# Second stage of an MLP: the first product's half units dealt out over all groups of the seven-product stage, and that stage's last block product placed among the direct end's first products

## The chip, the core and the metric

The kernel runs on one core of one Trainium2 chip. The metric is the device time of one execution in microseconds. The change touches the last third of the kernel, the MLP; everything ahead of it is the same in both versions.

## The reference, cut to what matters

One layer of a hybrid encoder, 256 tokens of width 2048, in float32: a mixer (two kinds of attention and an RWKV branch) with a residual, and then the MLP that this case is about. Its hidden width is 8192.

```python
x = x + _rms_norm(mix, norm_mix_post[l])
hdn = jnp.square(jax.nn.relu(_rms_norm(x, norm_mlp_pre[l]) @ w_mlp_up[l]))
x = x + _rms_norm(hdn @ w_mlp_down[l], norm_mlp_post[l])
```

`w_mlp_up` is 2048 x 8192, `w_mlp_down` 8192 x 2048.

## The kernel before, in words

**Splitting.** Every weight tile is 128 x 1024 floats (512 KB). It is fetched by the SP queue into a buffer `raw` (tag `raw`, three buffers, for the first product) or `raw2` (six buffers, for the blocks), then split in two: `ScalarE` copies it, rounded, to `whi` (line 152), and `VectorE` subtracts that from the tile to give the rest, `wlo` (line 153). `whi` and `wlo` have three buffers each. After a group or so every fourth tile is split into a spare tile `sp` instead (lines 1074 and 1075), and every seventh block is loaded into a spare tile. TensorE multiplies with the high and the low part.

**First product.** The hidden width is cut into 64 units of 128. A unit takes two weight tiles; its work on one of them is a half unit: eight products with `whi` and eight narrower ones with `wlo` (`gemm`, lines 168, 172 and 176). After the second half, `post` (lines 1101 to 1111) empties the PSUM tile and applies relu and the square.

**Second product.** The units go in five blocks, SIZES = (12, 16, 16, 12, 8), FIRST = (0, 12, 28, 44, 56). Blocks 0 to 3 are multiplied by the seven-product scheme for 2 x 2 block matrices (Winograd's form of Strassen's): in place of eight block products there are seven, named F1 to F7, and sums of blocks. For this the hidden values are brought into seven forms (`forms`, lines 1131 to 1142), and the weight blocks are summed on the way: two such sums are made by VectorE (line 1168) and two by a transfer that adds to its destination, issued by GpSimd (`dma_add`, line 1171). Each of the seven block products takes one split tile and the forms of two pairs of units; on TensorE it is six matmuls (lines 1209 to 1211). The seven over two pairs of units (four units) and one half of the output width are called a group here: blocks 0 to 3 have 3, 4, 4 and 3 groups for each of the two output halves, 28 groups in all, numbered 0 to 27 in this text. Results go from PSUM into `y` by short VectorE additions (line 1216).

The last block, units 56 to 63, is multiplied directly (`tok`, lines 198 and 214): the direct end. Its hidden values are only split (`split3`, lines 1153 and 1154). It reads 16 weight tiles, and ends with the second norm and the residual: `x1`, read back from DRAM (`xs`), is added and written out.

**Order.** Units 0 to 11 are made before group 0. The other 52 units are made during the groups, one block ahead of their use. A list `work` is written by hand; `drive` takes its items one by one, and prepares (`prep`: loads, splits, sums) two items further on than the one that TensorE runs. An item's number says how many small waiting tasks (forms, sums into `y`) go out behind it. In a group the order is F3, half, F4 of the group before, forms that are due, F7, F1, half, F6, F2, half, F5, half. F4 is put off by a group's half because its tile is the one that the second adding transfer makes: loaded tile `R22` is used by F3, F7 and F6 and summed in between, and then `dma_add(R22, R21)` gives F4's tile.

Every group takes two units, four halves, as long as there are any. 52 units are 26 groups' worth, so groups 26 and 27 have none; in them the seven products' items send out one task each. F4 of group 27 (`last4`) is run at the end, and then the first tiles of the direct end are loaded (`first3`). The four gains and the four parts of `x1` are fetched one by one behind the direct end's first weight tiles (list `side`). `x1` lies in the buffers of the two spare tiles, so it can be fetched when these are no longer needed.

In the MLP a scheduler places each engine's instructions by their priority in this order and by what they need; each engine then works its list in order. SP's list too is worked in order: a transfer that has to wait holds those behind it.

```python
for it in (F[3], us[0], last4, "old", F[7], F[1], us[1], F[6], F[2], us[2], F[5], us[3]):
```

Of the kernel before, what the change touches and what calls it, by code (L numbers as in the profile page):

```python
# [10 lines left out]
F32 = mybir.dt.float32  # L11
# [7 lines left out]
D = 2048  # L19
# [31 lines left out]
def hybrid_block(ctx, tc, xt, x, gains, params, consts, lora, gup, wst, out):  # L51
    nc = tc.nc
# [12 lines left out]
    def nm(s):  # L65
        uid[0] += 1
        return f"{s}_{uid[0]}"
# [7 lines left out]
    def pk():  # L75
        return pkpool.tile([128, 512], F32R, tag="pk", name=nm("pk"), bufs=24)
# [20 lines left out]
    threads = []  # L97
# [4 lines left out]
    def start(gen):  # L102

        threads.append({"gen": gen, "need": None, "due": clock[0]})
# [36 lines left out]
    side = []  # L141
# [109 lines left out]
    def g1(w=T):  # L251
        return rp.tile([128, T], F32, tag="g1", name=nm("g1"), bufs=20)
# [46 lines left out]
    for h in range(2):  # L299
        w = {}  # L300
        for k in range(8 * h, 8 * h + 8):
            xsplit(k)
            i = k - 8 * h
            if i in (0, 3, 5):
                j = len(w)
# [537 lines left out]
    for hf in range(2):  # L843
        for s, mo in (("k", MU_K), ("r", MU_R), ("v", MU_V)):
            for p in range(4 * hf, 4 * hf + 4):
                ps = unit(upk)
                d = g1()
# [33 lines left out]
    for g in range(4):  # L881
        m = rp.tile([128, 2, 512], F32, tag="m", name=nm("m"), bufs=4)
        m = [m[:, 0], m[:, 1]]
# [25 lines left out]
    for g in range(4):  # L909
        if g < 3:  # L910
            branch(ycp, thc[g], ms[g], False)
        else:
            m = [pk().bitcast(F32) for _ in range(2)]
# [6 lines left out]
    p2 = ctx.enter_context(tc.tile_pool(name="p2", bufs=1))  # L920
# [23 lines left out]
    x1 = [p2.tile([128, D], F32, tag="x1", name=nm("x1"), bufs=2) for _ in range(2)]  # L944
    for c in range(0, D, 512):
        for tt in range(2):
            loads.append(lambda tt=tt, c=c: nc.sync.dma_start(out=x1[tt][:, c:c + 512],
                                                              in_=x[tt * 128:tt * 128 + 128, c:c + 512]))
# [42 lines left out]
    for k2 in range(0, KT, 2):  # L991
# [7 lines left out]
        for i in range(2):  # L999
            u = pk()  # L1000
# [15 lines left out]
    xs = [dp.tile([128, D], F32, name=nm("xs")) for _ in range(2)]  # L1016
    AF_ = {1: 0, 2: 1, 4: 2, 7: 3, 5: 4, 6: 5, 3: 6}
    SIZES = (12, 16, 16, 12, 8)
    FIRST = [sum(SIZES[:b]) for b in range(5)]
    work, urgent, tasks, hl = [], [], [], {}  # L1020
    ahead, spare, made, kinds, units = [AHEAD], [], [0], [0], [0]

    def emit(n):

        while n and tasks:
            tasks.pop(0)[1]()
            n -= 1
# [226 lines left out]
    def later(new):  # L1254
        return (None, lambda _: urgent.append(lambda: tasks.extend(new)), 0)
# [12 lines left out]

    LAST = FIRST[4] // 2
    old = []  # L1270
    nxt, last4 = SIZES[0], None
    m_new = SIZES[0] // 2
    left = {m: 0 for m in range(m_new, 8)}
    for b in range(4):
        for sb in range(2):
            for d, F in enumerate(down(b, sb)):
                us = []
                while len(us) < 2 and nxt < FIRST[4] + SIZES[4]:
                    us.append(up(nxt))
                    nxt += 1  # L1280
                us = [u for pair in us for u in pair] + [None] * 4
                if not us[0]:
                    F = {f: it[:2] + (1,) for f, it in F.items()}
                for it in (F[3], us[0], last4, "old", F[7], F[1], us[1], F[6], F[2], us[2], F[5], us[3]):
                    if it == "old":
                        keep = []
                        for m in old:
                            if m in left:
                                work.append(later(split3(m) if m >= LAST else forms(m)))
                            else:  # L1290
                                keep.append(m)
                        old[:] = keep
                    elif it:
                        work.append(it)
                if us[3]:
                    old.append(nxt // 2 - 1)
                last4 = F[4]
                if sb:
                    for m in (2 * d, 2 * d + 1):
                        left[FIRST[b] // 2 + m + 8] = 0  # L1300
    work.append(last4)

    def first3():
        order[:] = [base + 3 * 64 + 32 + 8 * g + k for g in range(4) for k in range(4, 8)]
        for _ in range(1 + AHEAD):
# [4 lines left out]
        work.append(later(split3(m)))  # L1310
    work.append((None, lambda _: first3(), 0))
    drive()
    spare.clear()
    x1 = [p2.tile([128, D], F32, tag="x1", name=nm("x1"), bufs=2) for _ in range(2)]

    hp = [hp[k] for k in range(FIRST[4], FIRST[4] + SIZES[4])]
    g4, loads = gain(1, [pk() for _ in range(4)])
    side.extend(loads)
    for tt in range(2):
        side.extend(lambda tt=tt, c=c: nc.sync.dma_start(out=x1[tt][:, c:c + 1024], in_=xs[tt][:, c:c + 1024])  # L1320
                    for c in (0, 1024))
    for g in range(4):
        gs = slice(512 * g, 512 * g + 512)
        for tt, ps in enumerate(tok(hp, 3 if g == 3 else 1)):
            yv = ys[tt][:, gs]
            V.tensor_tensor(yv, yv, ps, ALU.add)
            A.activation(junk(), yv, AF.Square, accum_out=ss4[:, tt, g:g + 1])

            def gained():
                V.tensor_tensor(yv, yv, g4[g], ALU.mult)  # L1330

            if g < 3:
                gained()
                if g == 2:
                    sum4.append(rstd_of(ss4[:, tt, :], eps4[tt], None))
            else:
                r4 = rstd_of(ss4[:, tt, :], None, sum4[tt])
                gained()
                for c in range(0, D, 512):
                    cs = slice(c, c + 512)  # L1340
                    V.scalar_tensor_tensor(x1[tt][:, cs], ys[tt][:, cs], r4, x1[tt][:, cs], ALU.mult, ALU.add)  # L1341
                    nc.sync.dma_start(out=out[tt * 128:tt * 128 + 128, cs], in_=x1[tt][:, cs])
# [125 lines left out]
```

## Time and profile before

| | |
|---|---|
| median of three runs | 1549.11 us (1543.35 to 1551.61) |
| profiled execution | 1545.02 us |
| its span | 1543.2 us |
| TensorE busy | 1506.6 us, 98% |
| VectorE busy | 1194.7 us, 77% |
| ScalarE busy | 918.5 us, 60% |
| read from memory | 281.86 MB |

The profile is of one execution; the 1.8 us between its time and its span lie outside the recorded instructions. In its rows PE is TensorE's matmuls, PEld its weight loads, DVE VectorE, ACT ScalarE, POOL GpSimd, SP the engine that issues most transfers; SPq and POOLq are queues of transfers. L168 is line 168. `mps<-whi,fm` is a matmul that writes a tile `mps` and reads `whi` and `fm`. A row of the timeline has the start in us from the span's start, the duration, the engine, the line, what was written and read, how many there are in the row, and in brackets how long the engine had been idle and what ended that.

In the seven-product stage (about 930 to 1485 us) TensorE's matmuls follow each other without a gap up to 1463 us. Matmuls are pipelined, so that one of 0.39 us starts every 0.23 us.

### The profile page before, as it was taken

How to read it: one execution, taken by the hardware profiler on the slowest of the kernel's cores; microseconds unless marked ns; L12 is line 12 of the kernel's file. 1: busy time of each engine (PE TensorE's matmuls, PEld its weight loads, DVE VectorE, ACT ScalarE, POOL GpSimd, SP SyncE). 2: the span in 40 equal slices, each digit the busy share in tenths (PEclk: the TensorE clock that was granted, in tenths of full speed). 3: DMA queues.
4: the chain of work that ended last, by engine and by line, in shares of the span. 5: the costliest groups of instructions: out<-in, count | busy, mean ns of one | idle time of the engine just before them, and what ended most of it. 6: DMA issues, size and time to landing. Idle time of an engine off the chain costs nothing.

```text
span 1543.2 us, 22386 instructions
## 1 busy us (share of the span) xinstructions
PE 1506.6 (98%) x8294; PEld 1264.1 (82%) x8294; DVE 1194.7 (77%) x1608; ACT 918.5 (60%) x1340; POOL 91.1 (6%) x163
## 2 busy tenths in 40 slices
PE   7999999999999999999999999999999999999987
PEld 6888888888777788788887888888888888888865
DVE  6865567788548798447655878999899989998975
ACT  7564566554546554455444766777667776776642
POOL 0021000000000100000000000000000000000000
PEclk9999999999999999999999999999999999999999
DMA  7545455545534445435785658888888887889864
GB/s 259 189 165 175 153 178 178 167 147 187 176 121 141 160 160 192 154 125 180 241 304 178 232 173 249 250 260 247 255 254 256 254 263 228 255 253 273 255 191 137
DMA packets 105117, 316.88 MB, mean 205 GB/s; under 512 B 10288, under 2 KB 12720, under 8 KB 104624
## 3 DMA queue, kind: packets, MB, share of 16 engines
q1 hardware_dynamic: 93536, 282.76, 53.4%
q0 software_dynamic: 8064, 29.36, 10.3%
q10 hardware_dynamic: 3408, 3.34, 0.6%
q8 instruction: 65, 1.06, 0.3%
q14 instruction: 44, 0.36, 0.1%
HBM read 281.86 MB, written 4.19 MB: 185 GB/s over the span
## 4 chain that ended last, share of the span: by engine, by line
PE 47%; issue 5%; DMA 2%; DVE 1%; ACT 1%; POOL 0%; POOLq 0%; DVEq 0%; ACTq 0%
PE gps L168 12%; PE gps L214 10%; PE gps L172 7%; PE gps L198 3%; PE mps L1209 3%; PE mps L1210 3%; PE mps L1211 3%; PE gps L1209 2%; PE gps L1211 2%; PE gps L1210 2%; DMA raw<-in_wst_dram 1%; PE gps L176 1%; DMA sp<-raw 0%; DMA raw<-sp 0%; DVE x L1341 0%
## 5 line engine op out<-in xcount | busy, mean ns | idle before, releaser
L153 DVE TENSOR_TENSOR wlo<-raw,whi 128x1024 fp32r<-128x1024 f32 x505 | 613.5, 1222 | 193.8 <-ACT whi L152 176.2
L152 ACT ACTIVATE whi<-raw 128x1024 fp32r<-128x1024 f32 x505 | 532.0, 1057 | 273.9 <-PE gps L214 122.8
L168 PE MATMUL gps<-pk,whi 128*128 128x512 f32 x1301 | 330.9, 393 | 0.1
L214 PE MATMUL gps<-whi,pk 128*128 128x512 f32 x1144 | 291.3, 394 | 0.0
L168 PEld LDWEIGHTS gps<-pk,whi 128*128 128x128 f32 x1301 | 241.3, 188 | 48.2 <-issue 0.9
L214 PEld LDWEIGHTS gps<-whi,pk 128*128 128x128 f32 x1144 | 213.6, 188 | 45.6 <-issue 1.0
L172 PEld LDWEIGHTS gps<-pk,wlo 128*128 128x128 f32 x1391 | 190.1, 190 | 14.5 <-issue 1.2
L172 PE MATMUL gps<-pk,wlo 128*128 128x256 f32 x1391 | 195.8, 283 | 0.0
L214 PE MATMUL gps<-wlo,pk 128*128 128x512 f32 x572 | 157.4, 394 | 0.0
L214 PEld LDWEIGHTS gps<-wlo,pk 128*128 128x128 f32 x572 | 106.9, 188 | 23.2 <-issue 0.7
L1075 DVE TENSOR_TENSOR sp<-raw,sp 128x1024 fp32r<-128x1024 f32 x69 | 84.2, 1220 | 3.9 <-ACT sp L1074 3.7
L1101 ACT ACTIVATE sp<-gps 128x512 f32<-128x512 f32 x52 | 31.1, 598 | 88.2 <-PE gps L176 88.1
L1074 ACT ACTIVATE sp<-raw 128x1024 fp32r<-128x1024 f32 x69 | 72.9, 1056 | 16.0 <-PE mps L1210 7.0
L1209 PE MATMUL mps<-whi,fm 128*128 128x512 f32 x168 | 67.0, 399 | 6.9 <-ACT whi L152 6.9
L198 PE MATMUL gps<-whi,pk 128*128 128x512 f32 x264 | 71.9, 393 | 0.0
L1211 PE MATMUL mps<-wlo,fm 128*128 128x512 f32 x168 | 66.2, 394 | 0.8 <-DVE wlo L153 0.8
L1210 PE MATMUL mps<-whi,fm 128*128 128x512 f32 x168 | 66.3, 395 | 0.0
L1171 POOL DMA_DIRECT2D raw<-raw x40 | 35.0, 874 | 439.7 <-DVE raw L1168 137.8
L198 PEld LDWEIGHTS gps<-whi,pk 128*128 128x128 f32 x264 | 49.3, 188 | 10.5 <-ACT whi L152 0.2
L1209 PE MATMUL gps<-whi,fm 128*128 128x512 f32 x126 | 49.3, 391 | 0.0
L1168 DVE TENSOR_TENSOR raw<-raw,raw 128x1024 f32<-128x1024 f32 x40 | 48.8, 1220 | 0.4
L1211 PE MATMUL gps<-wlo,fm 128*128 128x512 f32 x126 | 49.1, 391 | 0.0
(342 smaller groups left out, 1964.9 us busy)
## 6 DMA issues: line engine op xcount, KB each, us to landing
raw<-in_wst_dram SPq DMA_DIRECT2D x502, 512.0 KB, 4.3
raw<-raw POOLq DMA_DIRECT2D x40, 512.0 KB, 6.1
sp<-in_wst_dram SPq DMA_DIRECT2D x16, 512.0 KB, 5.4
raw<-sp POOLq DMA_DIRECT2D x8, 512.0 KB, 6.5
sp<-raw POOLq DMA_DIRECT2D x8, 512.0 KB, 6.9
x<-in_x_dram SPq DMA_DIRECT2D x8, 256.0 KB, 5.9
xs<-x SPq DMA_DIRECT2D x2, 1024.0 KB, 4.0
x<-xs SPq DMA_DIRECT2D x4, 512.0 KB, 5.4
```

The source lines that it names most:

```text
L152: A.activation(hi, raw, AF.Copy)
L153: V.tensor_tensor(lo, raw, hi.bitcast(F32), ALU.subtract)
L168: PE.matmul(ps, hi[:, i * 128:i * 128 + 128], pks[i], start=first and i == 0, stop=False)
L172: PE.matmul(ps[:, 0:T], lo[:, i * 128:i * 128 + 128], pks[i][:, 0:T], start=False, stop=False)
L198: PE.matmul(ps[tt], pks[k][:, c:c + 128], w[:, (k - k0) * 512:(k - k0) * 512 + 512], start=k == 0 and part == 0 and w is hl[0], stop=w is ...
L214: PE.matmul(ps[tt], pks[k][:, c:c + 128], w[:, (k - k0) * 512:(k - k0) * 512 + 512], start=k == 0 and part == 0 and w is hl[0], stop=False)
L1074: A.activation(hi, raw, AF.Copy)
L1075: V.tensor_tensor(lo, raw, hi.bitcast(F32), ALU.subtract)
L1168: V.tensor_tensor(x, x, z, ALU.add)
L1209: PE.matmul(Q[f], p, w, start=d == 0 and i == 0, stop=False)
L1210: PE.matmul(Q[f], pl, w, start=False, stop=False)
L1211: PE.matmul(Q[f], p, wl, start=False, stop=d == nd - 1 and i == 1)
```

## The change

There are as many half units as before (104), and as many of all other instructions. A list `share` says how many halves each group takes: four in the first 18 groups, then 3, 3, 3, 3, 4, 4, 3, 4, 3, 2. So a unit can begin in one group and end in the next; its forms are due in the group after its second half. In the last group all items send out a task.

`last4` is no longer run ahead of the direct end: a thread (`end4`) that advances with the direct end's own count of time prepares it some 3.5 us into the direct end, runs it 3 us later, and sends out its sums into `y` after another 2 us. The spare tiles stay in use until then, and `x1` is fetched in one piece of the program ahead of the direct end's third quarter.

```diff
--- before.py
+++ after.py
@@ -1268,19 +1268,19 @@
 
     LAST = FIRST[4] // 2
     old = []
-    nxt, last4 = SIZES[0], None
-    m_new = SIZES[0] // 2
-    left = {m: 0 for m in range(m_new, 8)}
+    last4 = None
+    left = {m: 0 for m in range(SIZES[0] // 2, 8)}
+    halves = [(h, j) for j in range(SIZES[0], FIRST[4] + SIZES[4]) for h in up(j)]
+    share = [4] * 18 + [3, 3, 3, 3, 4, 4, 3, 4, 3, 2]
+    assert sum(share) == len(halves)
+    halves_of = {j: (h, j) for h, j in halves}
     for b in range(4):
         for sb in range(2):
             for d, F in enumerate(down(b, sb)):
-                us = []
-                while len(us) < 2 and nxt < FIRST[4] + SIZES[4]:
-                    us.append(up(nxt))
-                    nxt += 1
-                us = [u for pair in us for u in pair] + [None] * 4
-                if not us[0]:
-                    F = {f: it[:2] + (1,) for f, it in F.items()}
+                us = [halves.pop(0) for _ in range(share.pop(0))]
+                new = [j // 2 for i, (u, j) in enumerate(us) if j % 2 and (u, j) == halves_of[j]]
+                us = [u for u, j in us] + [None] * 4
+                last = b == 3 and sb == 1 and d == SIZES[3] // 4 - 1
                 for it in (F[3], us[0], last4, "old", F[7], F[1], us[1], F[6], F[2], us[2], F[5], us[3]):
                     if it == "old":
                         keep = []
@@ -1291,15 +1291,12 @@
                                 keep.append(m)
                         old[:] = keep
                     elif it:
-                        work.append(it)
-                if us[3]:
-                    old.append(nxt // 2 - 1)
+                        work.append(it[:2] + (1,) if last and it[2] == 0 else it)
+                old.extend(new)
                 last4 = F[4]
                 if sb:
                     for m in (2 * d, 2 * d + 1):
                         left[FIRST[b] // 2 + m + 8] = 0
-    work.append(last4)
-
     def first3():
         order[:] = [base + 3 * 64 + 32 + 8 * g + k for g in range(4) for k in range(4, 8)]
         for _ in range(1 + AHEAD):
@@ -1310,17 +1307,31 @@
         work.append(later(split3(m)))
     work.append((None, lambda _: first3(), 0))
     drive()
-    spare.clear()
-    x1 = [p2.tile([128, D], F32, tag="x1", name=nm("x1"), bufs=2) for _ in range(2)]
+
+    def end4():
+        yield 3.5
+        hl = last4[0]()
+        yield 3.0
+        last4[1](hl)
+        while urgent:
+            urgent.pop(0)()
+        yield 2.0
+        emit(-1)
+
+    start(end4())
 
     hp = [hp[k] for k in range(FIRST[4], FIRST[4] + SIZES[4])]
     g4, loads = gain(1, [pk() for _ in range(4)])
     side.extend(loads)
-    for tt in range(2):
-        side.extend(lambda tt=tt, c=c: nc.sync.dma_start(out=x1[tt][:, c:c + 1024], in_=xs[tt][:, c:c + 1024])
-                    for c in (0, 1024))
     for g in range(4):
         gs = slice(512 * g, 512 * g + 512)
+        if g == 2:
+            assert not threads
+            spare.clear()
+            x1 = [p2.tile([128, D], F32, tag="x1", name=nm("x1"), bufs=2) for _ in range(2)]
+            for tt in range(2):
+                for c in (0, 1024):
+                    nc.sync.dma_start(out=x1[tt][:, c:c + 1024], in_=xs[tt][:, c:c + 1024])
         for tt, ps in enumerate(tok(hp, 3 if g == 3 else 1)):
             yv = ys[tt][:, gs]
             V.tensor_tensor(yv, yv, ps, ALU.add)
```

Three places where the order of instructions moved. The first is ScalarE's list in group 26, from the split for F7 on (L152 and L1074 are splits; `raw_13465`, `raw_13493`, `raw_13430` and the like are loaded blocks; L1101, L1107 and L1111 belong to `post`, L1153 to `split3`). Before:

```order
L152 ACTIVATE whi_13467<-sp_8489 128x1024
L1101 ACTIVATE sp_8489<-gps_13410 128x512
L1074 ACTIVATE sp_8488<-raw_13465 128x1024
L1107 ACTIVATE tmp_13479<-tmp_13479 128x256
L152 ACTIVATE whi_13495<-sp_8489 128x1024
L1111 ACTIVATE pk_13393<-tmp_13479 128x256
L1153 ACTIVATE fm_13506<-pk_13203 128x256
L152 ACTIVATE whi_13509<-raw_13493 128x1024
L1153 ACTIVATE fm_13519<-pk_13203 128x256
L152 ACTIVATE whi_13522<-raw_13430 128x1024
L1153 ACTIVATE fm_13532<-pk_13393 128x256
L1074 ACTIVATE sp_8488<-raw_13535 128x1024
```

With the change:

```order
L152 ACTIVATE whi_13352<-sp_8489 128x1024
L1074 ACTIVATE sp_8488<-raw_13350 128x1024
L1101 ACTIVATE sp_8489<-gps_13321 128x512
L152 ACTIVATE whi_13390<-raw_13388 128x1024
L1107 ACTIVATE tmp_13383<-tmp_13383 128x256
L152 ACTIVATE whi_13402<-sp_8489 128x1024
L1111 ACTIVATE pk_13313<-tmp_13383 128x256
L152 ACTIVATE whi_13413<-raw_13400 128x1024
L1074 ACTIVATE sp_8488<-raw_13440 128x1024
L1153 ACTIVATE fm_13559<-pk_13313 128x256
L1153 ACTIVATE fm_13572<-pk_13313 128x256
L152 ACTIVATE whi_13450<-raw_13297 128x1024
```

Before, the only splits are those of F7, F1, F6, F2, F5 and the next group's F3; now the splits of half units, `raw_13388` and `raw_13440`, stand between them.

The second is TensorE's list where the seven products end and the direct end (L214) begins. Before, with F4 of group 27 in `mps_13486`:

```order
L1209 MATMUL mps_13486<-whi_13617,fm_12608 128x512
L1210 MATMUL mps_13486<-whi_13617,fm_12611 128x512
L214 MATMUL gps_13668<-whi_13645,fm_12998 128x512 x2
L1211 MATMUL mps_13486<-wlo_13618,fm_12608 128x512
L1209 MATMUL mps_13486<-whi_13617,fm_12898 128x512
L1210 MATMUL mps_13486<-whi_13617,fm_12941 128x512
L1211 MATMUL mps_13486<-wlo_13618,fm_12898 128x512
L214 MATMUL gps_13669<-whi_13645,fm_12998 128x512 x2
L214 MATMUL gps_13668<-whi_13645,fm_13001 128x512 x2
L214 MATMUL gps_13669<-whi_13645,fm_13001 128x512 x2
```

With the change, with F4 of group 27 in `mps_13376`:

```order
L214 MATMUL gps_13654<-whi_13670,fm_13559 128x512 x2
L214 MATMUL gps_13655<-whi_13670,fm_13559 128x512 x2
L214 MATMUL gps_13654<-whi_13670,fm_13572 128x512 x2
L214 MATMUL gps_13655<-whi_13670,fm_13572 128x512 x2
L1209 MATMUL mps_13376<-whi_13681,fm_12829 128x512
L1210 MATMUL mps_13376<-whi_13681,fm_12832 128x512
L1211 MATMUL mps_13376<-wlo_13682,fm_12829 128x512
L1209 MATMUL mps_13376<-whi_13681,fm_12893 128x512
L1210 MATMUL mps_13376<-whi_13681,fm_12896 128x512
L1211 MATMUL mps_13376<-wlo_13682,fm_12893 128x512
L214 MATMUL gps_13654<-wlo_13671,fm_13559 128x512
L214 MATMUL gps_13655<-wlo_13671,fm_13559 128x512
```

F4 stood around the direct end's first matmuls (x2: two equal rows); now it stands in the middle of the direct end's third tile (`whi_13670`, `wlo_13671`), behind 32 of its matmuls.

The third is SP's list of transfers at the same place (L145 the direct end's weight tiles, L1064 blocks, L928 gains, L1320 and L1334 `x1`; `sp_8489` is the block R21 of group 27, loaded into a spare tile). Before:

```order
L145 DMA raw_13682<-in_wst_dram 128x1024
L928 DMA pk_13664<-in_gains_dram 128x512
L928 DMA pk_13665<-in_gains_dram 128x512
L1064 DMA raw_13561<-in_wst_dram 128x2x512
L928 DMA pk_13666<-in_gains_dram 128x512
L928 DMA pk_13667<-in_gains_dram 128x512
L1064 DMA sp_8489<-in_wst_dram 128x2x512
L1320 DMA x_2554_13662<-xs_7783 128x1024 x2
L1320 DMA x_2555_13663<-xs_7784 128x1024 x2
L145 DMA raw_13701<-in_wst_dram 128x1024
L145 DMA raw_13720<-in_wst_dram 128x1024
```

With the change:

```order
L145 DMA raw_13632<-in_wst_dram 128x1024
L928 DMA pk_13650<-in_gains_dram 128x512
L1064 DMA sp_8489<-in_wst_dram 128x2x512
L928 DMA pk_13651<-in_gains_dram 128x512
L928 DMA pk_13652<-in_gains_dram 128x512
L928 DMA pk_13653<-in_gains_dram 128x512
L145 DMA raw_13668<-in_wst_dram 128x1024
L1334 DMA x_2587_13828<-xs_7783 128x1024 x2
L145 DMA raw_13691<-in_wst_dram 128x1024
L145 DMA raw_13716<-in_wst_dram 128x1024
L1334 DMA x_2588_13829<-xs_7784 128x1024 x2
L145 DMA raw_13747<-in_wst_dram 128x1024
```

The four parts of `x1` (two rows of two) stood in one piece behind the direct end's third weight tile, with thirteen tiles behind them; now the first two stand behind the third tile and ahead of the fourth and fifth, and the other two behind those.

## The prediction

> **What bounds the kernel now.** I read the page's head first, then the busy time by stretches, then TensorE's waits, and last the chain of waits and the timeline at the place that these name.
>
> ```profile
> span 1543.2 us, 22386 instructions
> PE 1506.6 (98%) x8294; PEld 1264.1 (82%) x8294; DVE 1194.7 (77%) x1608; ACT 918.5 (60%) x1340; POOL 91.1 (6%) x163
> L153 DVE TENSOR_TENSOR wlo<-raw,whi 128x1024 fp32r<-128x1024 f32 x505 | 613.5, 1222 | 193.8 <-ACT whi L152 176.2
> L1168 DVE TENSOR_TENSOR raw<-raw,raw 128x1024 f32<-128x1024 f32 x40 | 48.8, 1220 | 0.4
> ```
>
> TensorE is the bound of the whole: a change that moves no work off it can win only where it waits. The next rows, from the busy time by stretches, have TensorE, its weight loads, VectorE, ScalarE and GpSimd (time and count), and then the granted clock, the transfer engines' share and GB/s.
>
> ```profile
> 1290.00:1455.00 165.00, 165.00 (x848) 141.30 (x847) 154.84 (x181) 115.24 (x154) 13.93 (x16) 1.00 0.86 251
> 1357.00:1378.00 21.00, 21.00 (x109) 17.98 (x108) 21.00 (x27) 15.14 (x22) 1.74 (x2) 1.00 0.77 224
> 1290.00:1491.00 201.00, 193.00 (x951) 161.75 (x950) 184.49 (x214) 133.04 (x177) 16.54 (x19) 0.98 0.84 244
> 1464.00:1491.00 27.00, 19.04 (x65) 13.37 (x66) 22.78 (x27) 11.04 (x13) 1.74 (x2) 0.87 0.67 184
> ```
>
> From 1290 to 1455, groups 18 to 25, TensorE never pauses though VectorE is busy 94% of the time. From 1464 to 1491, groups 26 and 27 and the first tile of the direct end, TensorE does 65 matmuls in 27 us. All its waits in the MLP from 950 us on are these:
>
> ```profile
> PE mps L1209 <- ACT whi L152: 6.9, 3, 4.2
> PE mps L1211 <- DVE wlo L153: 0.8, 2, 0.5
> PE mps L1209 <- ACT sp L1074: 0.2, 1, 0.2
> ```
>
> ScalarE is named, but the chain of waits says what ScalarE waited for: three transfers.
>
> ```profile
> 1459.71 7.06 DMA sp<-raw
> ...
> 1469.22 4.55 DMA sp<-in_wst_dram
> ...
> 1477.62 5.26 DMA raw<-sp
> ...
> 1482.97 1.06 ACT whi L152
> ```
>
> So in groups without half units, the blocks' loads and the adding transfers come too late: a block product gives TensorE little to do while VectorE splits and sums its tile. The timeline of TensorE shows what a product, a half unit and the long wait cost:
>
> ```profile
> 1448.24 1.98 PE L168 MATMUL gps<-pk,whi 128*128 128x512 f32 x8
> ...
> 1451.01 0.40 PE L1209 MATMUL mps<-whi,fm 128*128 128x512 f32 x1
> ...
> 1452.39 1.75 PE L168 MATMUL gps<-pk,sp 128*128 128x512 f32 x7
> ...
> 1484.07 0.80 PE L1209 MATMUL mps<-whi,fm 128*128 128x512 f32 x1 [4.22 <-ACT whi L152]
> ...
> 1490.78 1.99 PE L214 MATMUL gps<-whi,fm 128*128 128x512 f32 x8
> 1492.61 1.07 PE L214 MATMUL gps<-wlo,fm 128*128 128x512 f32 x4
> 1493.51 0.84 PE L214 MATMUL gps<-whi,fm 128*128 128x512 f32 x3
> ```
>
> A half unit takes 1451.01 - 1448.24 = 2.77 us, a block product 1.38 us. Unhindered, twelve matmuls take 1493.51 - 1490.78 = 2.73 us, 0.2275 each. So 65 would take 14.8 us, and the stretch loses 27.0 - 14.8 = **12.2 us**. Of these 7.9 are the waits listed. Another 2.6 are the slow clock after the longest of them: between 1484.07 and 1490.78 TensorE runs the direct end's first tile and group 27's F4, 18 matmuls, in 6.7 us where 4.1 would do. The remaining 1.7 is the refilling of the matmul pipeline after the waits.
>
> **The change, part by part.** *Half units.* Nothing is added or removed; five halves go from groups 18 to 25 to groups 26 and 27. TensorE's work is the same, and each group's time on it is 7 x 1.38 + 2.77 for each half: 20.7 us with four, 18.0 with three, 15.2 with two, against 9.7 with none. With at least 15.2 us for it, the chain of a group's loads and sums has time again, so the waits go: up to -12.2 us.
>
> What it costs: in a group with three or two halves the work of the seven products comes denser. On VectorE that is nine operations of 1.22 us (seven splits, two sums). The missing half between F5 and the next F3 gave TensorE 2.77 us of work and VectorE one split of 1.22, so it let VectorE get 1.5 us further ahead. How far ahead it is shows where the end of a split is set against the first matmul that reads its low part (VectorE's rows, then TensorE's):
>
> ```profile
> 1398.56 1.22 DVE L1075 TENSOR_TENSOR sp<-raw,sp 128x1024 fp32r<-128x1024 f32 x1
> 1441.40 1.22 DVE L1075 TENSOR_TENSOR sp<-raw,sp 128x1024 fp32r<-128x1024 f32 x1
> 1449.55 1.22 DVE L153 TENSOR_TENSOR wlo<-sp,whi 128x1024 fp32r<-128x1024 f32 x1
> ```
>
> ```profile
> 1400.43 0.39 PE L1211 MATMUL gps<-sp,fm 128*128 128x512 f32 x1
> 1455.63 0.40 PE L1211 MATMUL gps<-wlo,fm 128*128 128x512 f32 x1
> 1457.00 0.39 PE L1211 MATMUL mps<-wlo,fm 128*128 128x512 f32 x1
> ```
>
> F3 of group 26 has 1455.63 - 1450.77 = 4.9 us in hand; F1 of group 23, behind both sums, has 1400.43 - 1399.78 = 0.65, the least I found. With 1.5 less, F3 keeps 3.4, and an F1 like that one is 0.9 late. Six groups have three halves and one has two: from nothing to 7 x 0.9, 0 to 6 us given back. I take 2.5, nearer to nothing: that F1 was the worst one, and only the part of the 1.5 counts that isn't made up before F1. The two-half group has the direct end's products in place of its last halves.
>
> *Forms and splits of the hidden values* move with their units; they are as many, on VectorE and ScalarE, and lie in the sum above. The last unit's `split3` now stands right ahead of the direct end, which needs it only in its fourth tile, three tiles (8.2 us) later: 0.
>
> *The last block product.* Its six matmuls only change their place: 0 on TensorE. It no longer holds the direct end, and the 4.22 us wait and the slow clock behind it go; they are part of the 12.2. Its tile's adding transfer is started when F6 of group 27 is split. From F6 to the product there are F6, F2, F5 and 32 matmuls of the direct end: 3 x 1.38 + 7.3 = 11.4 us. The transfer (5.26 us in the chain above) and the two halves of the split (1.06 and 1.22) need 7.5: hidden, with 3.9 us in hand. Queued behind this split on ScalarE and VectorE is that of the direct end's fourth tile, 0.9 us of matmuls later: if the transfer takes more than 9 us, both are late.
>
> *`x1`.* As many transfers, at another place in SP's list: two of them, and all tiles behind them, now wait for that last adding transfer ahead of the direct end's fourth weight tile.
>
> ```profile
> DMA to landing us min/median/max: 5.2/6.4/10.7
> ...
> raw<-in_wst_dram SPq DMA_DIRECT2D x10, 512.0 KB, 4.1
> x<-xs SPq DMA_DIRECT2D x4, 512.0 KB, 5.4
> ```
>
> The first row is of the adding transfers from 930 to 1460 us, the others of 1470 to 1510. TensorE needs the fourth tile's low part 13.7 us after F6 begins (11.4, F4's 1.38, and 0.9 of products with its high part). The adding transfer lands some 5.3 us after F6 was split, so 8.4 are left, 6.1 without the split. With the two `x1` transfers ahead the tile takes 5.4 us beside them and 5.4 + 4.1 = 9.5 behind them: 0 to 3.4 us late. I take 0: the four `x1` transfers too were issued in one piece, and took 5.4 us each, not four times as long in turn. The gains and the tail after TensorE's last matmul stay: 0.
>
> The Trainium skill speaks against this place: "DMA: Bandwidth & Descriptors", section "Issuing engines are not separate DMA queues", says that transfers started by SP and by GpSimd run on the same 16 engines and interleave. By that the adding transfer would share them with the direct end's tiles and `x1`, as in the busy stretch, where rows above have 10.7 us as the longest; the gain would be some 3 us less, 1542. In the trace the chain's three transfers (4.55 to 7.06) show no such length.
>
> **Sum:** -12.2 + 2.5 = -9.7 us. The profiled execution took 1545.0 us, 4.1 less than the median of the three runs; the sum makes it 1535.3, and the median 1549.1 - 9.7 = **1539.4**. All of the gain would be 1536.9.
>
> **Rivals.** *VectorE becomes the bound.* From 1290 to 1491 it is busy 184.5 of 201 us; without 12.2 the same work stands in 188.8, 98%. For it: no stretch here holds 98% for so long. Against it: 21 us at 100% (second row of the stretches) without a wait. If 94%, its share while TensorE ran freely, is all that goes, the work takes 184.5 / 0.94 = 196.3 us: a gain of 4.7, 1544.4.
>
> *The direct end waits for its fourth tile* behind `x1` or the last split, by up to the 3.4 us above: 12.2 - 2.5 - 3 = 6.7, 1542.4.
>
> *The other side: the adding transfers end last in every short group.* F4's tile is complete when `R21` has been added. In group 25 the transfer could start when F6 was split, at 1442.62, and F4 read its low part at 1457.00: 14.4 us. With one half less between them 11.6 are left, less 2.3 for the split: 9.3 for the transfer. Median 6.4 speaks against a wait; a longest of 10.7, and the denser traffic, for one. A group with four halves moves about 20.7 x 251 = 5.2 MB; a half less is 0.52 MB less, so 4.7 MB in 18.0 us, 260 GB/s. Each us above 9.3 costs the seven short groups 7 us. From a mean of 10.7 on, the 9.7 are lost; at 11.3, 14 - 9.7 = 4.3 us slower, 1553.4; at 11.8, 7.8 slower.
>
> **How the numbers follow.** The forecast 0.64; VectorE as the bound 0.20; the fourth tile 0.08; the adding transfers 0.08, of which 0.05 slower by over 0.5%. The range takes the full gain from the fastest of the three runs, 1543.35 - 12.2 = 1531, and goes up past the VectorE rival to 1547. About 0.5%, 7.7 us, is what a measurement of this kernel can tell from no change. Of the forecast's 0.64, 0.04 give back 4.5 us or more and lie within it; so faster 0.60, within 0.35, slower 0.05.
>
> **What would show it.** Right: no waits of TensorE over 1 us between 1290 us and the end of the direct end, no dip of its clock there, the direct end's first matmul straight behind F5, and a span 8 to 12 us shorter. Wrong: waits at `wlo` in F1 of the three-half groups with VectorE full (first rival); a wait at the direct end's fourth tile with SP held (second); waits at F4 with ScalarE waiting for an adding transfer (third).

## The result, and the profile after

The changed kernel took 1533.1 us (median of six runs, 1531.5 to 1534.5) beside 1548.6 of the kernel before: a ratio of 0.9907, 95% interval 0.9893 to 0.9922, 14.4 us faster. On a second occasion it was 1534.2 beside 1545.9, ratio 0.9923 (0.9909 to 0.9937), 11.7 us. The profiled execution took 1534.53 us.

The head of the page of after:

```profile
span 1532.8 us, 22383 instructions
PE 1503.2 (98%) x8294; PEld 1262.6 (82%) x8294; DVE 1192.7 (78%) x1608; ACT 917.8 (60%) x1340; POOL 91.0 (6%) x163
```

The span is 10.4 us shorter; all engines have the same instructions as before. Two of the stretches that the prediction showed, in after:

```profile
1290.00:1455.00 165.00, 164.16 (x829) 139.09 (x828) 156.88 (x184) 116.27 (x155) 14.99 (x18) 1.00 0.87 253
1464.00:1491.00 27.00, 27.00 (x129) 22.63 (x128) 23.54 (x29) 14.81 (x20) 0.87 (x1) 1.00 0.85 294
```

In the last row 129 matmuls stand where there were 65; the granted clock is 1.00 where it was 0.87, and the transfer engines carry 294 GB/s where they carried 184. TensorE's waits in the MLP are two:

```profile
PE gps L1211 <- DVE wlo L153: 0.4, 1, 0.4
PE mps L1211 <- DVE sp L1075: 0.4, 1, 0.4
```

TensorE's timeline where the direct end begins shows the last F5, the direct end's first tile straight behind it, and F4 of group 27 in the middle of its third, at full speed:

```profile
1476.03 0.39 PE L1211 MATMUL mps<-wlo,fm 128*128 128x512 f32 x1
1476.26 1.98 PE L214 MATMUL gps<-whi,fm 128*128 128x512 f32 x8
...
1483.96 0.39 PE L1211 MATMUL mps<-wlo,fm 128*128 128x512 f32 x1
...
1486.68 0.62 PE L198 MATMUL gps<-wlo,fm 128*128 128x512 f32 x2
```

Where the two waits of 0.4 come from: F2 of group 20 (1339.19) waited for a block that was loaded into the spare tile in 7.98 us, F1 of group 21 (1352.33) for VectorE's own row of a sum and a split. The chain of waits of after, and then VectorE's row behind that block:

```profile
1328.75 7.98 DMA sp<-in_wst_dram
...
1339.19 0.50 PE mps L1211
...
1349.92 1.22 DVE raw L1168
1351.14 1.15 DVE wlo L153
...
1352.33 0.50 PE gps L1211
```

```profile
1337.91 1.23 DVE L1075 TENSOR_TENSOR sp<-sp,sp 128x1024 fp32r<-128x1024 f32 x1 [3.96 <-ACT sp L1074]
```

VectorE had stood 3.96 us for that same block, and then worked almost without a pause (12.70 of the 13 us from 1340 us) up to the second wait.

The theory after the result: the gain is the loss between 1464 us and the end of the direct end's first tile, taken away by the two parts together; what is given back in the short groups is given back through transfers that come late. Rivals: VectorE's load sets what is given back; the last product's place alone brings the gain; part of the 14.4 us lies outside what the profiles show, which have 10.4.

### The profile page after: what moved, and what is told of

It is laid out like the page before. It is cut to its first block, busy times and chain, and to the rows that moved or that the text cites. A ratio compares the mean times of both kernels' runs of the same rounds, so it can differ in the third digit from the quotient of the medians.

```text
span 1532.8 us, 22383 instructions
## 1 busy us (share of the span) xinstructions
PE 1503.2 (98%) x8294; PEld 1262.6 (82%) x8294; DVE 1192.7 (78%) x1608; ACT 917.8 (60%) x1340; POOL 91.0 (6%) x163
## 4 chain that ended last, share of the span: by engine, by line
PE 53%; DVE 1%; DMA 1%; ACT 1%; issue 0%; POOL 0%; DVEq 0%; POOLq 0%; ACTq 0%
PE gps L168 14%; PE gps L214 10%; PE gps L172 8%; PE mps L1209 3%; PE mps L1210 3%; PE mps L1211 3%; PE gps L198 3%; PE gps L1211 2%; PE gps L1209 2%; PE gps L1210 2%; PE gps L176 1%; DMA sp<-in_wst_dram 1%; DVE x L1352 0%; DVE wlo L153 0%; ACT junk L1113 0%
## 5 line engine op out<-in xcount | busy, mean ns | idle before, releaser
L152 ACT ACTIVATE whi<-raw 128x1024 fp32r<-128x1024 f32 x507 | 533.9, 1057 | 276.0 <-PE gps L214 107.7
L214 PE MATMUL gps<-whi,pk 128*128 128x512 f32 x1144 | 291.5, 394 | 0.0
L214 PEld LDWEIGHTS gps<-whi,pk 128*128 128x128 f32 x1144 | 213.7, 188 | 45.8 <-issue 1.0
L214 PE MATMUL gps<-wlo,pk 128*128 128x512 f32 x572 | 157.4, 394 | 0.0
L214 PEld LDWEIGHTS gps<-wlo,pk 128*128 128x128 f32 x572 | 106.9, 188 | 23.2 <-issue 0.7
L1074 ACT ACTIVATE sp<-raw 128x1024 fp32r<-128x1024 f32 x67 | 70.7, 1055 | 14.9 <-PE mps L1211 3.9
L1101 ACT ACTIVATE sp<-gps 128x512 f32<-128x512 f32 x52 | 31.1, 597 | 80.7 <-PE gps L176 80.7
L1209 PE MATMUL mps<-whi,fm 128*128 128x512 f32 x168 | 66.2, 394 | 0.0
L198 PEld LDWEIGHTS gps<-whi,pk 128*128 128x128 f32 x264 | 49.3, 188 | 10.6 <-ACT whi L152 0.2
L1209 PE MATMUL gps<-whi,fm 128*128 128x512 f32 x126 | 49.2, 391 | 0.0
```

Of the source, the lines that this page charges most:

```text
L152: A.activation(hi, raw, AF.Copy)
L198: PE.matmul(ps[tt], pks[k][:, c:c + 128], w[:, (k - k0) * 512:(k - k0) * 512 + 512], start=k == 0 and part == 0 and w is hl[0], stop=w is ...
L214: PE.matmul(ps[tt], pks[k][:, c:c + 128], w[:, (k - k0) * 512:(k - k0) * 512 + 512], start=k == 0 and part == 0 and w is hl[0], stop=False)
L1074: A.activation(hi, raw, AF.Copy)
L1209: PE.matmul(Q[f], p, w, start=d == 0 and i == 0, stop=False)
```

## Experiments

The first four kernels ran beside 1547.4 us of the kernel before, the next four beside 1545.9, the last three, on a third occasion, beside 1545.9. All ratios are to the kernel before of the same occasion. The place of `x1` is as in the change in all of these kernels but the kernel before; no run moves `x1` alone.

**One part alone: the half units spread, the last product ahead of the direct end.**

```diff
+    work.append(last4)
...
-    start(end4())
```

(The body of `end4` goes too.)

> Half units spread as in the change, but the last block product F4 stays ahead of the direct end. Theory: it has to wait there for its adding transfer. From the start of F6 to F4 there are three products, 4.1 us; the transfer (5.3 us in the trace of before) and the split (2.3) need about 7.5. So one wait of about 3.5 us and, if the clock drops again, 2 to 3 us of slow matmuls behind it: about 1539 us, ratio to before 0.993 to 0.995, 4 to 6 us slower than the changed kernel. Rival: with half units in every group all transfers come in time, and the place of the last product is worth nothing: like the changed kernel, 1533 us, 0.991, and no wait of TensorE ahead of the direct end.

1537.5 us, ratio 0.9934 (0.9922 to 0.9947). Its waits of TensorE:

```profile
PE gps L214 <- DVE wlo L153: 0.7, 1, 0.7
PE gps L168 <- DVE junk L1216: 0.6, 1, 0.6
PE mps L1211 <- DVE wlo L153: 0.5, 1, 0.5
```

The ratio is what was expected, but not for the reason given. F4 of group 27 waited 0.5 us; no long wait for its adding transfer came, and no slow clock. With two halves in group 27 the transfer starts early enough even for a product that stands ahead of the direct end: it went out at 1470.5 us, and ScalarE split its tile at 1475.6.

**The other part alone: the last product moved, groups 26 and 27 without halves.**

```diff
-    share = [4] * 18 + [3, 3, 3, 3, 4, 4, 3, 4, 3, 2]
+    share = [4] * 26 + [0, 0]
...
-                last = b == 3 and sb == 1 and d == SIZES[3] // 4 - 1
+                last = not us[0]
```

> Halves as before (none in groups 26 and 27), but the last block product among the direct end's first products. Theory: the waits inside groups 26 and 27 stay (about 3.6 us named in the trace of before, 5 with the refilling of the pipeline), the long one of 4.2 us and the slow clock behind it (2.6) go: about 7 us faster than before, 1541 us, 0.9955, with the adding transfer landing while the direct end's tiles are multiplied. Rival: the long wait only moves, because the last product's split stands in ScalarE's and VectorE's lists ahead of the direct end's fourth tile and its transfer starts as late as before: a wait in the third or fourth tile of the direct end, and 0 to 3 us faster than before, 0.998 to 1.000.

1539.6 us, ratio 0.9950 (0.9937 to 0.9962), near the theory's 1541 and 0.9955.

```profile
PE mps L1209 <- ACT whi L152: 3.3, 3, 1.8
PE mps L1211 <- DVE wlo L153: 1.1, 2, 0.5
PE mps L1209 <- ACT sp L1074: 0.2, 1, 0.2
```

And its last stretch, with columns as before:

```profile
1464.00:1491.00 27.00, 22.76 (x93) 16.93 (x94) 23.64 (x27) 14.38 (x17) 1.74 (x2) 1.00 0.74 210
```

The wait of 4.2 us is gone and with it the slow clock (the clock is 1.00); the waits inside groups 26 and 27 stay, 4.6 us in all.

**Two halves in each of the last four groups**, in place of six groups of three and one of two:

```diff
-    share = [4] * 18 + [3, 3, 3, 3, 4, 4, 3, 4, 3, 2]
+    share = [4] * 24 + [2] * 4
```

> The change with the same 104 halves dealt otherwise: four in groups 0 to 23, two in each of groups 24 to 27. Theory: VectorE has more than a two-half group's 15.2 us of work, so that what it is ahead (3 to 5 us at F3) is used up in four such groups in a row: waits at low parts of F7, F1 and F6 in groups 25 to 27, 2 to 5 us in all, 1535 to 1538 us, 0.992 to 0.994. Rival: only whole groups without halves are too thin, any halves do: like the changed kernel, 1533 us, 0.991, no waits over 0.5 us.

1539.6 us, ratio 0.9947 (0.9934 to 0.9959), slower than either expectation: the waits are there. Its TensorE waits, and two of its stretches:

```profile
PE mps L1211 <- DVE sp L1075: 1.2, 2, 0.7
PE gps L1211 <- DVE sp L1075: 1.2, 2, 1.0
PE mps L1209 <- ACT sp L1074: 0.3, 1, 0.3
PE mps L1209 <- ACT whi L152: 0.3, 1, 0.3
```

```profile
1443.00:1459.00 16.00, 16.00 (x79) 13.49 (x79) 15.76 (x18) 11.13 (x15) 1.74 (x2) 1.00 0.88 240
1459.00:1476.00 17.00, 15.37 (x72) 11.82 (x71) 13.96 (x15) 9.82 (x14) 1.74 (x2) 1.00 0.75 205
```

Of the 3.0 us of waits, 1.2 (the second row) lie at 1378 and 1401 us, in groups that still have four halves; the others lie from 1437 to 1475. While VectorE is full (15.76 of 16 us, first row) TensorE doesn't wait; 1.6 us of the waits lie in the stretch after that, where VectorE has pauses. There ScalarE stood for transfers:

```profile
ACT sp L1074 <- DMA sp<-raw: 4.1, 1, 4.1
ACT whi L152 <- DMA sp<-in_wst_dram: 2.5, 1, 2.5
```

**The same number of short groups, with a full group between them where there is room.**

```diff
-    share = [4] * 18 + [3, 3, 3, 3, 4, 4, 3, 4, 3, 2]
+    share = [4] * 18 + [3, 4, 3, 4, 3, 4, 3, 3, 3, 2]
```

> The change with the three-half groups apart where the order of the units allows it: 3, 4, 3, 4, 3, 4, 3, 3, 3, 2 in groups 18 to 27. Theory: the two waits of 0.4 us left in the changed kernel's trace (groups 20 and 21) come from three-half groups in a row; apart they go, 1 to 1.5 us, 1532 us, 0.990. Rival: they come from one late load (8 us for a block into the spare tile), whatever the neighbours: the same time as the changed kernel, and a like wait somewhere.

1534.8 us, ratio 0.9910 (0.9895 to 0.9925), no different from the change. Two waits again, of 0.4 and 0.3 us, at 1414 and 1451 us (F1 of groups 24 and 26): they moved with the short groups and didn't go. A split of VectorE ends each, but the chain of waits goes back to an adding transfer each time:

```profile
1396.53 10.26 DMA raw<-raw
...
1434.22 9.35 DMA raw<-raw
```

So the theory fails; the rival is right in the time and in that a late transfer begins the wait, but it is not always the load of one block.

**VectorE or the transfers?** Both on the kernel with two halves in each of the last four groups, there alone (`short` is true in groups 24 to 27). First without VectorE's two sums:

```diff
-            h0 = FIRST[b] + 4 * d
+            h0, short = FIRST[b] + 4 * d, b == 3 and (sb == 1 or d == 2)
...
-                add(R[d, "22"], R[d, "12"])
+                short or add(R[d, "22"], R[d, "12"])
...
-                add(R[d, "22"], R[d, "11"])
+                short or add(R[d, "22"], R[d, "11"])
```

> As the kernel with two halves in each of the last four groups, with the two sums that VectorE makes of the weight blocks left out in those four groups (eight operations of 1.22 us, 9.8 us of VectorE; its output is not the reference's). That kernel's profile has TensorE waits of 0.2 to 0.7 us in groups 26 and 27, 1.6 in all, behind a stretch (1427 to 1459 us) in which VectorE was busy 99% of the time; at the waits ScalarE stood 4.1 us for an adding transfer and 2.5 us for a loaded block. Theory: the transfers set these waits; they stay, 1 to 2 us in all, the time is 1538 to 1540, at most 1 us less than with the sums. Rival: VectorE, full, sets them; with a tenth of its work gone TensorE waits for nothing in the last four groups, and the time is 1536 to 1538.

1541.4 us, ratio 0.9962 (0.9950 to 0.9974): not faster, and slower than either expectation. The two longest of its waits, and then the stretch in which they lie:

```profile
PE mps L1209 <- ACT whi L152: 1.8, 1, 1.8
PE gps L1209 <- ACT whi L152: 1.7, 1, 1.7
```

```profile
1427.00:1443.00 16.00, 11.96 (x49) 9.07 (x48) 9.97 (x12) 7.86 (x11) 0.05 (x1) 0.86 0.77 211
```

VectorE is busy 62% of that stretch, and TensorE waits longer than with the sums (4.6 us in all from 950 us on, against 3.0). The timeline of GpSimd and the chain of waits say why:

```profile
1403.32 0.87 POOL L1171 DMA_DIRECT2D sp<-raw  x1 [8.81 <-issue]
1403.87 1.22 POOL L1171 DMA_DIRECT2D raw<-raw  x1
1424.87 1.77 POOL L1171 DMA_DIRECT2D raw<-raw  x2 [19.78 <-DMA raw<-in_wst_dram]
```

```profile
1403.87 10.59 DMA raw<-raw
...
1425.42 9.83 DMA raw<-raw
```

The sums had kept the adding transfers apart: with them GpSimd's transfers go out 6.7 to 11.8 us after each other. A group's first adding transfer had to wait for a sum; without the sums it goes out right ahead of the second of the group before, the one that F4 waits for. That happens three times, and the second of the two takes 10.59, 9.83 and 9.37 us (the first 7.83, 5.53 and 7.41). The wait of 1.8 us stands at F4 of group 24, behind the 9.83. So this edit took load off VectorE and pushed transfers together, and the time followed the transfers; it is no test of VectorE's load alone.

Then with the sums and without the adding transfers:

```diff
-                dma_add(R[d, "12"], R[d, "11"])
+                short or dma_add(R[d, "12"], R[d, "11"])
...
-                dma_add(R[d, "22"], R[d, "21"])
+                short or dma_add(R[d, "22"], R[d, "21"])
```

> As the kernel with two halves in each of the last four groups, with the two adding transfers left out in those four groups (eight transfers of 512 KB that read and add; its output is not the reference's). VectorE's work is the same. Theory (the transfers set the waits in groups 26 and 27): ScalarE no longer waits for an adding transfer, the loads share the engines with less, and TensorE's waits from 1463 us on are under 0.3 us in all; 1536 to 1538. Rival (VectorE sets them): VectorE is still busy 98% or more from 1427 to 1459, and 1 to 2 us of waits stay, behind its splits; 1538 to 1540.

1534.7 us, ratio 0.9924 (0.9906 to 0.9942). All of TensorE's waits in the MLP, and two stretches:

```profile
PE mps L1209 <- ACT whi L152: 0.3, 1, 0.3
```

```profile
1427.00:1443.00 16.00, 15.69 (x76) 12.65 (x75) 16.00 (x18) 10.86 (x14) 0.00 (x0) 1.00 0.53 176
1443.00:1459.00 16.00, 16.00 (x80) 13.54 (x79) 15.97 (x19) 11.57 (x15) 0.00 (x0) 1.00 0.61 190
```

VectorE is busy 31.97 of 32 us, and TensorE waits 0.3 in all. That wait, in group 25, also stands in the kernel with the adding transfers, and here only a sum and a split lie behind it: it is what a full VectorE costs. The 1.6 us of waits from 1463 us on are the adding transfers', by their own length or by what they take from the loads: from 1400 to 1476 us the loads' median is 5.2 us with them and 4.5 without. This holds for the kernel with two halves in each of the last four groups; the changed kernel was not run without its adding transfers.

**The kernel before again, twice**, for the 4 us between 14.4 and 10.4:

> The kernel before, unchanged, with a new profile. The first profile was of an execution near the lowest of its times (1545.0 us, where the median is about 1548), and it lost 12.2 us from 1464 to 1491 us; the change was timed at 14.4 us faster. Theory: in its other executions the kernel before loses more at the same place, since it waits there for transfers that don't always take the same time, and TensorE's clock is lowered for some us behind each long wait. Its mean granted clock over an execution bears this out so far: 0.996 at 1544.7 us, 0.992 at 1549.1, 0.990 at 1549.6. If this profile's time is 1547 to 1550 us, the stretch from 1464 to the end of the direct end's first tile is longer than 27.0 us by about the time above 1545.0, 2 to 5 us, with a second wait of over 3 us or a longer slow clock in it, and all ahead of 1464 us is as long as in the first profile within 0.7 us. Rival: the surplus lies ahead of 1464 us, in the stages that the change doesn't touch; then it is no gain of the change, and the 14.4 us stay unexplained by 4.

> The kernel before, unchanged, profiled once more; as for the other repeat. Should both repeats lie near 1545 us, the question stays open.

1546.4 and 1544.1 us, so neither was as long as hoped. TensorE's timeline of the first at the first wait of the place and at the direct end's second tile; between them lies the long wait, 4.27 us here:

```profile
1466.31 0.50 PE L1211 MATMUL mps<-wlo,fm 128*128 128x512 f32 x1 [0.52 <-DVE wlo L153]
...
1492.18 1.98 PE L214 MATMUL gps<-whi,fm 128*128 128x512 f32 x8
```

The same stretch took 1490.78 - 1464.27 = 26.5 us in the first profile, 1492.18 - 1466.31 = 25.9 here, 26.4 in the other. The loss at this place is steady; the 1.4 us by which this execution is longer lie ahead of it (it arrives there 2.0 us later), so the theory is wrong in that point, and the rival right that the surplus lies ahead of 1464 us. But it is not all in stages that the change doesn't touch: of the 2.0 us, 0.4 lie ahead of the seven-product stage, and 0.53 are a wait of TensorE within it, in F2 of group 20. The second repeat waits there too, 0.85 us in two parts. In both, a block came late into the spare tile (the first repeat's row, then the second's):

```profile
1331.97 10.81 DMA sp<-in_wst_dram
```

```profile
1329.63 10.72 DMA sp<-in_wst_dram
```

This is the place of the changed kernel's wait in F2 of group 20, here with four halves in the group. The expectation's remark on the clock doesn't carry far: over 33 executions of the kernel before, the mean clock and the time go together only weakly (a correlation of -0.47).

**The change and both parts again, on one occasion.**

> The changed kernel, unchanged, timed beside the kernel before on another occasion and profiled again. So far it was timed at 14.4 us faster (12 to 16.6), while the two first profiles show 10.4 us less span, and the kernel before took 1548.6, 1547.4 and 1545.9 us (medians) on three occasions. Theory: the profiles show the gain as it is, TensorE's waits and the slow clock between 1463 us and the end of the direct end's first tile (10 to 12 us); the rest of the 14.4 was the occasion. Then the gain is 10 to 13 us here, and the profile of the changed kernel has waits of under 1 us in the MLP. Rival: the gain is 14 us or more again, and something of the kernel before that the profiles have not shown (its clock in other executions) adds to it.

> Only the half units spread, the last block product still ahead of the direct end, beside the whole change on the same occasion. The first time it was 4.4 us slower than the change had been on another occasion, though its profile shows only 1.0 us more of waits and 2.3 us more span. Theory: its surplus over the change is what the profile shows, 1 to 3 us. Rival: 4 us or more again; then the last block product's place is worth more than its waits.

> Only the last block product moved, the half units as before, beside the whole change on the same occasion. Its profile showed 4.6 us of waits and no slow clock behind them, and 4.7 us more span than the change. Theory: 4 to 6 us slower than the change, 5 to 8 us faster than the kernel before. Rival: less than 3 us from the change; then the spreading of the half units brings little, and most of the gain is the last product's place.

| | ratio (interval) | us saved | span of the profiles | from the first row of L1209 to TensorE's last row |
|---|---|---|---|---|
| the change | 0.9923 (0.9909 to 0.9937) | 11.7 | 1532.8, 1533.0 | 601.9, 602.0 |
| half units alone | 0.9938 (0.9925 to 0.9950) | 9.7 | 1535.1, 1533.3 | 604.1, 603.3 |
| last product alone | 0.9961 (0.9948 to 0.9974) | 6.2 | 1537.5, 1537.4 | 606.7, 606.6 |
| before | 1 | 0 | 1543.2, 1544.6, 1542.3 | 612.6, 613.6, 614.1 |

The theories hold in the times: 11.7 us lies within 10 to 13; the half units alone are 2.0 us behind the change (the intervals overlap), the last product alone 5.5. The last column, in us between the starts of the two rows, leaves out the stages that are the same in all four kernels; these differ by up to 2.8 us from profile to profile (the seven-product stage starts between 916.15 and 918.93 in the three of before). By its means the change gains 11.5 us, the half units alone 9.7 and the last product alone 6.8. The last is what the prediction gave for the long wait and the slow clock behind it, 4.2 + 2.6. The parts overlap (9.7 + 6.8 = 16.5): each takes away this wait and this slow clock. The new profile of the change has one wait in the MLP, in F1 of group 22 at 1370.50, just over the 1 us that was expected as the limit:

```profile
PE gps L1211 <- DVE wlo L153: 1.0, 1, 1.0
```

From 1337 to 1371 us VectorE was busy 32.56 of 34 us, behind a block that came late in group 20 again (ScalarE waited 3.20 us for it).

## Why the prediction was right, and where its sizes were off

*The bound and the place.* Right. TensorE's long waits lay between 1464 us and the direct end; those went, and so did the dip of the clock. That it waits nowhere else held for the first profile alone: the two repeats have 0.53 and 0.85 us in group 20. The span is 10.4 us shorter, of the 8 to 12 named as the mark. No wait of after from 1290 us on is over 1 us, but for the 1.04 of the second profile.

*The loss of 12.2 us.* Right, and steady: 26.5, 25.9 and 26.4 us for the same work in three profiles.

*Given back in the short groups: 2.5 us, 0 to 6.* Too large; this is the term of the sum that was mis-sized. By the last column of the table above the gain is 11.5 us, so 12.2 - 11.5 = 0.7 are given back. TensorE's rows agree: ahead of 1460 us after has 0.8 and 1.0 us of waits, but before has 0, 0.5 and 0.9 there, so about half a microsecond is new. The wait in F2 of group 20 comes with four halves too and is no cost of the short groups. Those in F1 stand where the prediction looked for them, behind VectorE's sums: in group 21, the last of four three-half groups in a row, and in group 22 right behind it. With the end of a split set against its first use as in the prediction, F1 of groups 22 and 23 had 0.1 us in hand in the first profile of after, where the worst of before had 0.65: the VectorE lead did shrink as argued, and mostly was just enough.

*The last product: "hidden, with 3.9 us in hand".* It was hidden, with 0.9; that the margin held was in part luck. The adding transfer was sized right (5.26 taken, 5.2 measured), but the two halves of the split did not start when it had landed. ScalarE's rows in after, and then VectorE's:

```profile
1478.27 1.06 ACT L152 ACTIVATE whi<-raw 128x1024 fp32r<-128x1024 f32 x1 [0.97 <-PE gps L214]
1483.47 1.06 ACT L152 ACTIVATE whi<-raw 128x1024 fp32r<-128x1024 f32 x1 [4.14 <-DMA raw<-in_wst_dram]
```

```profile
1481.27 0.68 DVE L1216 TENSOR_TENSOR y<-y,mps 128x512 f32<-128x512 f32 x1
1481.87 1.22 DVE L153 TENSOR_TENSOR wlo<-raw,whi 128x1024 fp32r<-128x1024 f32 x1
1484.56 2.51 DVE L153 TENSOR_TENSOR wlo<-raw,whi 128x1024 fp32r<-128x1024 f32 x2 [1.48 <-ACT whi L152]
```

The first half waited until the direct end's matmuls gave a `whi` buffer back (first row), the second stood on VectorE behind its list of additions into `y`, of which the first row is the last, until 1481.87. It ended at 1483.09, 0.87 us ahead of the matmul at 1483.96 above. The step that failed counted the transfer and the splits and left out the queue on VectorE and the buffer.

*`x1` ahead of the fourth tile: 0, of 0 to 3.4 us late.* Right, narrowly, and not by the times that it was argued from: the four `x1` transfers took a median of 7.4 us (5.4 had been assumed). ScalarE waited 4.14 us for that tile (second row above); its low part was ready at 1484.56 + 1.22 = 1485.78, and the matmul that reads it stands at 1486.68.

*The rivals.* VectorE as the bound of the stage fell with the time: it would have left 4.7 us of gain. In the kernel with two halves in each of the last four groups, TensorE's waits went with VectorE full and grew with VectorE 62% busy, the reverse of what this rival demands. What is left of it are the waits of 0.4 and 1.0 us in F1 of groups 21 and 22, which stand behind a full row of VectorE that followed a late block; whether the lost lead or the late block is to blame was not tried. The adding transfers do what the third rival said, short of the point from which it decides. From 1300 to 1460 us, the commonest of them, with their count, size and median us to landing, in the kernel before and in after:

```profile
raw<-raw POOLq DMA_DIRECT2D x11, 512.0 KB, 6.4
```

```profile
raw<-raw POOLq DMA_DIRECT2D x12, 512.0 KB, 8.2
```

Their median grew by 1.8 us in these two profiles; the repeats have 7.8 and 7.4 for before and 8.9 for after, so by 0.4 to 2.5, to below the 9.3 us that the rival named as its limit. The loads' median went from 5.9, 6.0 and 6.2 to 6.9 and 6.8. The Trainium skill ("DMA: Bandwidth & Descriptors", section "Issuing engines are not separate DMA queues") says that transfers share the same 16 engines whoever starts them. The traces agree: the loads' median fell from 5.2 to 4.5 us where the adding transfers were left out. For the last product's own transfer, for which the prediction weighed it, the 5.2 us show no such length.

*The time itself: 1539.4, measured 1533.1 and 1534.2.* Of the difference 1.8 us are the give-back (2.5 taken, 0.7 found). The rest is the base: the prediction subtracted from 1549.1, a median of three runs; the medians of the kernel before with more runs were 1548.6, 1547.4, 1545.9 and 1545.9. On the last of these occasions 1545.9 - 9.7 = 1536.2 stands 2.0 above the measured 1534.2, and 1545.9 - 11.5 = 1534.4 leaves next to nothing. The first occasion's 14.4 us is 2.9 more than the profiles show; the intervals of the two occasions (12.1 to 16.6 and 9.7 to 14.1) overlap, and no run shows a part of the kernel that would hold the surplus. That stays open.

## What to carry to other kernels

When a stage is fed by a chain of transfer, sum, transfer and split, look at how much work of the bounding engine lies between the start of a transfer and its use, stage by stage: independent work that is spread so that no stage runs out is worth more than its own waits, because it also keeps the clock up. A high busy share of an engine is a weak reason to expect it to be the next bound; leave out some of its work and some of its neighbour's in two runs, see which takes the waits away, and look in the trace whether the edit moved anything else. Profile the kernel before more than once: a wait that one profile lacks can be its own. When a step is moved behind other work, count the queue and the buffers that it will find there, not only its own duration.

## What the runs showed of the hardware that was not expected

When GpSimd started two adding transfers of 512 KB within 0.6 us of each other, the second took 9.4 to 10.6 us and the first 5.5 to 7.8 (three pairs, in the kernel without VectorE's sums). Started alone, 6.7 us or more apart, some take as long (10.26 us above), but the medians are 6.4 to 8.9.

TensorE's clock fell without a long wait. In these profiles the granted clock is 1.00 or 0.50, and changes only at the edges of stretches of 3.41 us. In the kernel without VectorE's sums waits of 1.82, 0.53 and 1.69 us stood within some six us. Two stretches there, one behind the other, and then one of the kernel with the last product alone:

```profile
1435.15:1438.56 3.41, 1.59 (x6) 0.97 (x6) 2.14 (x2) 3.23 (x4) 0.00 (x0) 1.00 0.51 151
1438.56:1441.97 3.41, 1.73 (x5) 1.04 (x4) 3.39 (x5) 2.10 (x3) 0.00 (x0) 0.50 0.87 331
```

```profile
1468.92:1472.34 3.42, 1.83 (x7) 1.22 (x8) 2.38 (x3) 2.90 (x3) 0.60 (x1) 1.00 0.71 134
```

TensorE was busy 1.59 of 3.41 us in the first, and the clock was at half in the next two. It was busy 1.83 of 3.42 us in the last, though a wait of 1.84 us ends in it, and the clock stayed at 1.00. In the kernel before, 1.73 of 3.41 us from 1472.24 left the clock at 1.00, and 0.79 from 1479.07 brought it down. So in this stage the busy share of such a stretch went with the clock, and the longest wait did not. A limit can't be read off: elsewhere in these traces, near 480, 840 and 1530 us, stretches that were busy about half the time went either way.
